# A hybrid RG-LRU and block-attention layer on one core: attention written out as a list of steps, with joined visits of TensorE

## The chip, the cores and the metric

The kernel runs on one NeuronCore of one Trainium2 chip. The metric is the device time of one execution in microseconds (us); the median of several runs is taken. Engines are named as in the profile: PE is TensorE, DVE is VectorE, ACT is ScalarE, POOL is GpSimd, SP is SyncE, which issues the DMAs.

## The reference, cut to what matters

One layer of a decoder for 512 tokens of width 1024, in float32:

```python
ada = silu(c) @ w_ada + b_ada;  shift, scale, gate = split(ada, 3)
h = rms_norm(x, norm_g) * (1 + scale) + shift
xl, gl, q, k, v, ga = split(h @ w_in, [512] * 6)
xl = causal_depthwise_conv(xl, conv_w, conv_b)
r = sigmoid(block_diag(xl, w_a) + b_a);  i = sigmoid(block_diag(xl, w_i) + b_i)
a = exp(-8 * r * softplus(-lam));  mult = sqrt(1 - a * a)       # mult[first token] = 1
h_t = a_t * h_(t-1) + mult_t * i_t * xl_t                        # the recurrence, a scan
y_lru = h_t * silu(gl)
q, k = rms_norm per head (8 heads of 64)
y_att = causal softmax attention(q, k, v) * silu(ga)
out = x + gate * (concat(y_lru, y_att) @ w_out)
```

The attention of the reference picks up to three past blocks of 256 keys for each query and its own block. With 512 tokens there are two blocks, so all past keys are always picked, and it is plain causal attention.

## The kernel before, in words

**Precision.** Each big product is made of three matmuls in the fast fp32 format: every operand is split into a high part (a copy, `split`, L272) and a low part (the difference), and high x high, high x low and low x high are summed in one PSUM bank.

**A planner sets the order.** The kernel doesn't issue instructions directly. Each step is an `op` (class `Plan`, L64) with a function that issues it, a cost in us for each engine that may run it, and the buffers that it reads and writes. `schedule` (L135) is a list scheduler: it repeatedly takes, among the steps whose inputs are done, the one that can start first; of those on the same engine that can start within `EPS_PICK` of it, the one with the smallest start plus `ALPHA` times due time. Due times come from the place of a TensorE step in the program text, and go backwards from each step to what it needs. A step that allocates a new SBUF slot may not start earlier than `window` (26 us) ahead of its due time; a step that writes into a slot which already exists has no such bound. Steps marked `bulk` (splits of weights) also leave ten of the 70 slots free. The planner keeps one more thing for TensorE: each step has a `mode` ("full" array, "row" for products on 64 rows, "col" for products on 64 columns, "col32"), and a step of another mode than the last is taken to start `SWITCH` later (L180). The order that comes out is the instruction order of every engine; semaphores do the rest at run time.

**PSUM.** There are eight banks. A step that opens a new use of a bank waits for every step of the bank's use before.

**Stages, in the order of TensorE.**
1. x is transposed and normed, ada is computed (TensorE for the first two k tiles, VectorE dot products for the six others, L443), h is made k tile by k tile from `gs` (L482 to L486) and split; xl and seven of eight tiles of the gates are accumulated over k (L515).
2. k, q and v for four token tiles (L617), with the RG-LRU gate products (L655) and the transposes of k and q (L724) in between. The RG-LRU chain behind the gate products (`gates`, L647 to L677): two tanh, an exp that gives a (L666), its square (L670), another tanh (L668), their product (L673); then `lru_sqrt` (L679), `lru_scan` (L685) and `lru_out` (L691).
3. Attention, for two pairs of query tiles a (a = 2 is the tiles 2 and 3, a = 0 the tiles 0 and 1) and four pairs of heads hp. `st_qk` (L748): S = q k^T for both heads of a pair at once, on the two row halves of the array, one step for each query tile, into banks 4 to 7. `softmax` (L773): mask and row maximum (L776, DVE), exp with row sum (L779, ACT), reciprocal (L782, DVE), scaling (L786 ACT, L788 POOL or DVE). `st_tr` (L792): transposes of P (L804) into banks 1 and 2 in turn, each copied out (pt). `st_pv` (L810): P v for both heads on the two column halves (L821), into bank 3; y = product with the attention gate (L824); after two head pairs y is split (ya).
4. In between as filler: five tiles of attention gates and the last RG-LRU gate (`g_tile`, L858), 24 matmuls each, in bank 0; the output gate's broadcast (`gate_bc`, L594), in bank 3.
5. The output product (`unit`, L830): for four token tiles and two halves of the columns, 24 matmuls each over y_lru (first 12) and y_att, then the multiplication by the gate, the residual and the store.

**The order of attention** before is a loop over six items (L917 to L940): the four head pairs of a = 2, then a = 0 in two items of two head pairs. Each turn puts S of the next item, one or two fills (a gate tile, and after the fourth item a unit), then the transposes and the pv of the item itself.

Of the kernel before, what the change touches and what calls it, by code (L numbers as in the profile page):

```python
# [29 lines left out]

NSLOT = 70
RESERVE = 10
SAME, SWITCH = 0.13, 0.1
EPS_PICK, ALPHA = 0.2, 0.1
NDV = 3
NPE = 2
# [27 lines left out]
class Plan:  # L64
# [70 lines left out]
    def schedule(self):  # L135
# [19 lines left out]
        while ready:  # L155
# [28 lines left out]
            if best is None:  # L184
# [1 line left out]
            s0, o0 = best  # L186
            e0 = o0.cand[0]
            o = min((r for r in ready if getattr(r, "cand", None) and r.cand[0] == e0 and r.cand[1] <= s0 + (EPS_PICK if s0 > T0 else EPS0)),
                    key=lambda r: r.cand[1] + (ALPHA if s0 > T0 else ALPHA0) * r.dl)
            for r in ready:  # L190
                if r is not o:
                    r.cand = None
# [46 lines left out]
def hybrid_layer_kernel(ctx: ExitStack, tc, x, small, call, bgate, wbd, wad, w1, wp, out):  # L239
# [23 lines left out]
        return op(fn, {"ACT": c_act(n, ap, psum), "DVE": c_dve(n, ap, psum, not psum)}, [src, *reads], [dst],  # L263
                  bulk=bulk, bias=bias)

    def tt(dst, d_ap, a, a_ap, b, b_ap, n, alu, psum=False, dve_only=False, rel=0.0):
        def fn(e):
            e.tensor_tensor(d_ap(), a_ap(), b_ap(), op=alu)  # L268
        costs = {"DVE": c_dve(n)} if psum or dve_only else c_tt(n)
        return op(fn, costs, [a, b], [dst], rel=rel)  # L270

    def split(src, s_ap, n, name, bulk=False, dve_only=False, rel=0.0):  # L272

# [157 lines left out]
    def load_ada(k):  # L431


        st = Buf(f"st{k}", "stage")
        for q in range(2):
            dma(lambda q=q: sp.dma_start(st.t[:, q * 1024:(q + 1) * 1024], wad[k, :, q * 1024:(q + 1) * 1024]), 0.5,
                [(st, q)], (DIP, 0.1, 0.1)[k] if k < 3 and q == 0 else 0.0)
        if k >= NPE:
            m = ada[k] = fixed(f"m{k}", [P, 2])
            for q in range(2):  # L440
                def dot(e, q=q):
                    v = st.t[:, q * 1024:(q + 1) * 1024]
                    dve.scalar_tensor_tensor(v, v, 1.0, cb.t, op0=MULT, op1=MULT, accum_out=m.t[:, q:q + 1])  # L443
                op(dot, {"DVE": c_dve(1024) + 0.15}, [cb], [(st, q), (m, q)])
            return
        acc = ada[k] = slot(f"ada{k}", n=256)
        part, p0 = (misc, 256) if k else (bank("adap0", 4), 0)

        def mm(q):
            for j in range(4):  # L450
                d = 4 * q + j
                pe.matmul(part.t[32 * j:32 * j + 32, p0:p0 + 256], csz.t[:, d, :], st.t[:, d * 256:(d + 1) * 256],
                          start=q == 0, stop=q == 1, tile_position=(0, 32 * j))
        key = (part, "sum")
# [16 lines left out]
    def gs_make(k):  # L471
        if k < NPE:
            acc = ada[k]

            def mm(e):
                for o in (0, 1):
                    pe.matmul(misc.t[:, 2 * k + o:2 * k + o + 1], acc.t[:, o * P:(o + 1) * P], ones.t[:, 0:1], start=True,
                              stop=True)
            op(mm, {"PE": 0.46}, [acc, ones], [(misc, k)], dl=T0 - 1.8 if k == 0 else T_[k] - 7.0)
        src = (misc, k) if k < NPE else ada[k]  # L480

        def mk(e):  # L482
# [164 lines left out]
    def gates(j, b_):  # L647
# [18 lines left out]
        op(lambda e: act.activation(aa_[j].t, tr.t, AF.Exp, bias=sn4.t[:, j:j + 1], scale=sn4.t[:, j:j + 1]),  # L666
           {"ACT": c_act(512, 2)}, [tr, sn4], [aa_[j]])
        op(lambda e: act.activation(t_.t, tr.t, AF.Tanh, bias=sp4.t[:, j:j + 1], scale=sp4.t[:, j:j + 1]),  # L668
           {"ACT": c_act(512, 2)}, [tr, sp4], [t_])
        tt(wv[j], lambda: wv[j].t, aa_[j], lambda: aa_[j].t, aa_[j], lambda: aa_[j].t, 512, MULT)  # L670

        def w_(e):
            dve.scalar_tensor_tensor(wv[j].t, wv[j].t, 1.0, t_.t, op0=ADD, op1=MULT)  # L673
            dve.memset(wv[j].t[:, 0:1], 1.0)
        op(w_, {"DVE": c_dve(512) + 0.07}, [t_], [wv[j]])
        op(lambda e: dve.scalar_tensor_tensor(ti[j].t, ti[j].t, 1.0, xc[j].t, op0=ADD, op1=MULT),
           {"DVE": c_dve(512)}, [xc[j]], [ti[j]])  # L677

    def lru_sqrt():  # L679
        def fn(e):  # L680
            for j in range(4):
                act.activation(wv[j].t, wv[j].t, AF.Sqrt, scale=1.0 / 16.0)
        op(fn, {"ACT": 4 * c_act(512) + 2.6}, [], [*wv])

    def lru_scan(j):  # L685
        w, c = wv[j], xc[j]
# [58 lines left out]
        ring.rotate(-1)  # L745
        return ring[-1]

    def st_qk(a, hps):  # L748

        for hp in hps:  # L750
            bb = {}
            for e_ in range(2):
# [1 line left out]
                    for t in (a + 1, a):  # L754
                        bb[t, e_] = (bank(f"S{t}{hp}{e_}", 4 + 2 * (t - a) + e_), 0)
                else:
                    b = bank(f"S{hp}{e_}", 4 + 2 * (hp - hps[0]) + e_)
                    bb[1, e_], bb[0, e_] = (b, 0), (b, 2 * P)
            for t in (a + 1, a):
                n = (t + 1) * P  # L760

                def fn(e, t=t, n=n, hp=hp, bb=bb):
                    for i, (x_, y_) in enumerate(((qTh, kTh), (qTh, kTl), (qTl, kTh))):
                        for e_ in range(2):
                            r, (b, c0) = slice(64 * e_, 64 * e_ + 64), bb[t, e_]
                            pe.matmul(b.t[:, c0:c0 + n], x_.t[r, hp, t * P:(t + 1) * P], y_.t[r, hp, 0:n],  # L766
                                      start=i == 0, stop=i == 2)
                op(fn, {"PE": c_mm(n, 3)}, [(qTh, t), (qTl, t)] + [(x_, i) for x_ in (kTh, kTl) for i in range(t + 1)],
                   [(bb[t, e_][0], t) for e_ in range(2)], mode="row")
                for e_ in range(2):  # L770
                    softmax(t, hp, e_, n, *bb[t, e_])

    def softmax(t, hp, e_, n, b, c0):  # L773
        st = fixed(f"st{t}{hp}{e_}", [P, 3])
        p_ = slot(f"P{t}{hp}{e_}")
        op(lambda e: dve.tensor_tensor_reduce(p_.t[:, :n], b.t[:, c0:c0 + n], maskf.t[:, 512 - n:], -1.0, -NEG,  # L776
                                              op0=ADD, op1=ALU.min, accum_out=st.t[:, 0:1]),
           {"DVE": c_dve(n) + 0.08}, [(b, t), maskf], [p_, (st, 0)])
        op(lambda e: act.activation(p_.t[:, :n], p_.t[:, :n], AF.Exp, bias=st.t[:, 0:1], scale=-1.0,  # L779
                                    accum_out=st.t[:, 1:2]),  # L780
           {"ACT": c_act(n, 2)}, [(st, 0)], [p_, (st, 1)])
# [28 lines left out]
    def st_pv(a, hp):  # L810
        if hp % 2 == 0:
            pv[a] = bank(f"pv{a}{hp}", 3)
            yy[a] = slot(f"y{a}{hp}")
        pt, b, y_, h0 = Tb.pop((a, hp)), pv[a], yy[a], 256 * (hp % 2)

        def fn(e):
            for kb in range(a + 2):
                n, o_ = (256, 0) if kb <= a else (128, 128)
                for e_ in range(2):
                    hd = 2 * hp + e_  # L820
                    pe.matmul(b.t[64 * e_:64 * e_ + 64, h0 + o_:h0 + o_ + n], vt[kb].t[:, hd * 64:(hd + 1) * 64],  # L821
                              pt[e_, kb // 2].t[:, 256 * (kb % 2):256 * (kb % 2) + n], start=kb == 0, stop=kb == a + 1)
        op(fn, {"PE": 0.26 + 0.435 * (a + 1)}, [*pt.values(), *vt[:a + 2]], [(b, hp)], mode="col")
        op(lambda e: dve.scalar_tensor_tensor(y_.t[:, h0:h0 + 256], b.t[:, h0:h0 + 256], 0.5,  # L824
                                              gga[hp].t[:, a * P:(a + 2) * P], op0=MULT, op1=MULT),
           {"DVE": c_dve(256)}, [(b, hp), gga[hp]], [(y_, hp)])
        if hp % 2 == 1:
            ya[a, hp // 2] = split(y_, lambda: y_.t, 512, f"ya{a}{hp}")
# [88 lines left out]
    items = [(2, (hp,)) for hp in range(4)] + [(0, (0, 1)), (0, (2, 3))]  # L917
    st_qk(*items[0])
    fill()
    for i in range(len(items)):  # L920
        if i + 1 < len(items):
            st_qk(*items[i + 1])
        fill()
        if i < 3:
            fill()
        if i == 2:
# [5 lines left out]
        a, hps = items[i]
        for hp in hps:
            st_tr(a, hp)
        for hp in hps:
            st_pv(a, hp)
        if i == 3:
# [87 lines left out]
```

## Time and profile before

| what | value |
|---|---|
| median of 3 runs | 237.19 us (237.05 to 237.79) |
| the profiled execution | 237.1 us |
| its span, first to last instruction | 235.3 us |
| granted clock of TensorE, mean | 0.998 |
| TensorE busy | 228.5 us, 97% of the span |
| VectorE busy | 173.0 us, 74% |
| ScalarE busy | 140.7 us, 60% |
| GpSimd busy | 55.4 us, 24% |
| HBM read, written | 35.43 MB, 2.10 MB |

How to read it: busy time is the time in which an instruction of the engine runs; a busy TensorE can still lose time between the starts of two matmuls, since matmuls are pipelined and their durations overlap. So its rate is read from the starts in the timeline. A group is a line of the kernel, an engine, an operation and its tiles, with the sum of its busy time and the mean of one. A wait is the idle time of an engine before an instruction, with what ended it. The stages lie at these times of the span: stage 1 until 56.5 us, k 56.5 to 81.9, q to 105.5, v to 129.9; attention with its fillers from 128.5 to 200.9; the rest of the output product until 232.1.

### The profile page before, as it was taken

How to read it: one execution, taken by the hardware profiler on the slowest of the kernel's cores; microseconds unless marked ns; L12 is line 12 of the kernel's file. 1: busy time of each engine (PE TensorE's matmuls, PEld its weight loads, DVE VectorE, ACT ScalarE, POOL GpSimd, SP SyncE). 2: the span in 40 equal slices, each digit the busy share in tenths (PEclk: the TensorE clock that was granted, in tenths of full speed). 3: DMA queues.
4: the chain of work that ended last, by engine and by line, in shares of the span. 5: the costliest groups of instructions: out<-in, count | busy, mean ns of one | idle time of the engine just before them, and what ended most of it. 6: DMA issues, size and time to landing. Idle time of an engine off the chain costs nothing.

```text
span 235.3 us, 3590 instructions
## 1 busy us (share of the span) xinstructions
PE 228.5 (97%) x1270; PEld 183.9 (78%) x1270; DVE 173.0 (74%) x399; ACT 140.7 (60%) x287; POOL 55.4 (24%) x56
## 2 busy tenths in 40 slices
PE   8799999999999999999999999999999999999994
PEld 8665888888878788888888778787777877788894
DVE  0778999979996767399745887597899894296221
ACT  5766555795487774342333399997998996140000
POOL 3300000000312844277020221447146320000001
PEclk9999999999999999999999999999999999999999
DMA  6999999958018005500654770001006031612411
GB/s 213 370 406 399 399 401 407 336 180 334 3 35 322 1 0 181 179 0 11 256 182 150 288 277 1 0 1 49 0 11 259 0 125 60 219 45 92 111 70 45
DMA packets 11879, 37.77 MB, mean 160 GB/s; under 512 B 1362, under 2 KB 3922, under 8 KB 9812
## 3 DMA queue, kind: packets, MB, share of 16 engines
q1 hardware_dynamic: 11860, 37.53, 44.2%
q8 instruction: 10, 0.16, 0.3%
q14 instruction: 9, 0.07, 0.1%
HBM read 35.43 MB, written 2.10 MB: 159 GB/s over the span
## 4 chain that ended last, share of the span: by engine, by line
PE 83%; DMA 9%; DVE 3%; ACT 2%; SPq 1%; issue 0%; DVEq 0%
PE u L843 19%; PE k L617 9%; PE g L867 9%; PE q L617 9%; PE xl L515 9%; PE gl L515 7%; PE v L617 6%; PE PT L804 4%; PE pv L821 4%; DMA st<-in_wad_dram 4%; DMA c<-in_call_dram 3%; PE S L766 3%; DVE ga L591 2%; DMA wg<-in_wp_dram 2%; PE pr L655 1%; ACT P L779 1%
## 5 line engine op out<-in xcount | busy, mean ns | idle before, releaser
L779 ACT ACTIVATE P<-P,st 128x512 f32<-128x512 f32 (+3 forms) x32 | 17.6, 556 | 3.5 <-DVE st L776 3.5
L268 DVE TENSOR_TENSOR o<-u,gbc 128x512 f32<-128x512 f32 (+1 forms) x8 | 5.3, 658 | 14.5 <-PE u L843 14.5
L788 POOL TENSOR_SCALAR P<-P,st 128x384 f32<-128x384 f32 (+3 forms) x13 | 9.0, 699 | 25.6 <-DVE st L782 25.6
L776 DVE CUSTOM_DVE_ANT_0 P<-S,maskf 128x512 f32<-128x512 f32 (+3 forms) x32 | 14.3, 481 | 0.9 <-PE g L867 0.9
L591 DVE SCALAR_TENSOR_TENSOR ga<-wg,cs,ga 128x512 f32<-128x512 f32 x16 | 12.8, 837 | 2.0 <-DMA wg<-in_wp_dram 2.0
L443 DVE SCALAR_TENSOR_TENSOR st<-st,cb 128x1024 f32<-128x1024 f32 x12 | 14.3, 1219 | 0.0
L268 POOL TENSOR_TENSOR xcs0l<-xc,xcs0h 128x512 fp32r<-128x512 f32 x1 | 1.3, 1294 | 50.6 <-ACT xcs0h L258 50.6
L258 ACT ACTIVATE pt<-PT 128x384 f32<-128x384 f32 (+1 forms) x23 | 11.1, 525 | 3.4 <-PE PT L804 3.2
L804 PE MATMUL PT<-ident,P 128*128 128x128 f32 x80 | 11.4, 277 | 0.3 <-ACT P L786 0.3
L804 PEld LDWEIGHTS PT<-ident,P 128*128 128x128 f32 x80 | 9.0, 141 | 3.1 <-issue 1.1
L821 PE MATMUL pv<-pt,vt 128*64 128x256 f32 (+1 forms) x96 | 10.0, 351 | 0.0
L786 ACT ACTIVATE P<-P,st 128x128 f32<-128x128 f32 (+3 forms) x19 | 9.5, 544 | 0.0
L496 ACT ACTIVATE hf<-xs,gs 128x512 f32<-128x512 f32 x8 | 6.5, 809 | 5.0 <-DVE gs L485 5.0
L712 POOL TENSOR_TENSOR msk<-msk,nhalf 128x8 f32<-128x8 f32 x4 | 6.6, 1647 | 12.3 <-DVE po L361 9.5
L821 PEld LDWEIGHTS pv<-pt,vt 128*64 128x64 f32 x96 | 6.4, 137 | 4.0 <-issue 1.2
L268 POOL TENSOR_TENSOR w_1l<-wp,w_1h 128x512 fp32r<-128x512 f32 x3 | 4.6, 1537 | 20.5 <-ACT w_1h L258 13.8
L268 DVE TENSOR_TENSOR w_0l<-wp,w_0h 128x512 fp32r<-128x512 f32 x11 | 8.1, 737 | 1.5 <-ACT w_0h L258 1.5
L258 ACT ACTIVATE qTh<-Tq 128x512 fp32r<-128x512 f32 x4 | 2.4, 598 | 11.3 <-PE Tq L724 11.3
L712 POOL TENSOR_TENSOR msq<-msq,nhalf 128x8 f32<-128x8 f32 x4 | 7.8, 1951 | 5.5 <-DVE msq L710 5.3
L268 POOL TENSOR_TENSOR o<-xr,o 128x256 f32<-128x256 f32 x1 | 0.7, 737 | 34.6 <-DVE o L268 34.6
L636 DVE SCALAR_TENSOR_TENSOR xc<-xl,sm,xc 128x511 f32<-128x511 f32 (+2 forms) x12 | 8.1, 740 | 0.3 <-ACT xc L633 0.3
L423 PE MATMUL warm<-warm 128*128 128x128 bf16 x72 | 6.6, 272 | 1.0 <-DVE warm L305 1.0
(719 smaller groups left out, 776.9 us busy)
## 6 DMA issues: line engine op xcount, KB each, us to landing
wp<-in_wp_dram SPq DMA_DIRECT2D x12, 1024.0 KB, 4.8
st<-in_wad_dram SPq DMA_DIRECT2D x16, 512.0 KB, 7.5
wg<-in_wp_dram SPq DMA_DIRECT2D x4, 1024.0 KB, 4.8
x<-in_x_dram SPq DMA_DIRECT2D x4, 512.0 KB, 6.0
wa<-in_w_dram SPq DMA_DIRECT2D x8, 256.0 KB, 7.7
xr<-in_x_dram SPq DMA_DIRECT2D x7, 256.0 KB, 2.9
out_dram<-o SPq DMA_DIRECT2D x7, 256.0 KB, 2.0
wb<-in_w_dram SPq DMA_DIRECT2D x8, 192.0 KB, 7.5
```

Of the source, the lines that this page charges most:

```text
L268: e.tensor_tensor(d_ap(), a_ap(), b_ap(), op=alu)
L443: dve.scalar_tensor_tensor(v, v, 1.0, cb.t, op0=MULT, op1=MULT, accum_out=m.t[:, q:q + 1])
L515: pe.matmul(acc.t, a.t[:, c0:c0 + P], b.t, start=k == 0 and i == 0, stop=k == KT - 1 and i == 2)
L591: dve.scalar_tensor_tensor(gacc[hf].t, w, cs.t[:, d:d + 1], gacc[hf].t, op0=MULT, op1=ADD)
L617: pe.matmul(acc.t, hx[kt].t[:, a * P:(a + 1) * P], wx.t, start=s0, stop=s1)
L712: op(lambda e: pool.tensor_tensor(m.t, m.t, nhalf.t, op=ALU.pow), {"POOL": 1.65}, [nhalf], [m])
L776: op(lambda e: dve.tensor_tensor_reduce(p_.t[:, :n], b.t[:, c0:c0 + n], maskf.t[:, 512 - n:], -1.0, -NEG, op0=ADD, op1=ALU.min, accum_out= ...
L779: op(lambda e: act.activation(p_.t[:, :n], p_.t[:, :n], AF.Exp, bias=st.t[:, 0:1], scale=-1.0, accum_out=st.t[:, 1:2]), {"ACT": c_act(n, 2 ...
L804: pe.transpose(b.t[:, o_:o_ + P], p_.t[:, kb * P:(kb + 1) * P], ident.t)
L821: pe.matmul(b.t[64 * e_:64 * e_ + 64, h0 + o_:h0 + o_ + n], vt[kb].t[:, hd * 64:(hd + 1) * 64], pt[e_, kb // 2].t[:, 256 * (kb % 2):256 * ...
L843: pe.matmul(b.t[:, :cn], y_.t[:, c0:c0 + P], w.t[:, cw:cw + cn], start=kt == 0 and i == 0, stop=kt == KT - 1 and i == 2)
L867: pe.matmul(b.t, wx.t[:, c0:c0 + P], hx[kt].t, start=kt == 0 and p == 0, stop=kt == KT - 1 and p == 2)
```

## The change

Four things, all in the kernel's text.

- **Attention as a list of steps.** The loop is replaced by a string `ORDER`. `S20` is a visit of S for a = 2 and head pair 0, `T20` the transposes of it, `P20` a pv visit, `P02+P03` two visits joined in one step. `F` is a fill in bank 0, `F3` a fill in bank 3. `G` is the broadcast of the output gate, `W` the end of the RG-LRU group and the loads of the output weights, `U` puts four units on the list of fillers. Fills that find nothing to do do nothing. The list was found off line by replaying plans.
- **Joined visits.** `st_qk` and `st_pv` become `qk_part` and `pv_part`, and `visit` makes one TensorE step of all their matmuls. S of both query tiles of a head pair is now one step (two before), and S of a = 0 is a visit of its own for each head pair, in banks 4 and 5 for even and 6 and 7 for odd pairs.
- **The RG-LRU chain opened ahead.** The exp and the square have a window of 200 us in place of 26; the second tanh overwrites `tr` in place of a new slot.
- **Costs of the planner.** `SWITCH` is 0.2 in place of 0.1. `TURN` adds 0.3 to the key of a TensorE step of another mode. The costs of the dots, the gate tanh, the square roots and the mask pass are set to traced durations. `gs` for k from 2 on runs on ScalarE (two one-column activations) in place of VectorE.

The diff, cut to its core:

```diff
+ORDER = ("S20 F3 S22 F F3 F3 S21 T20 T21 F3 P20 F S23 F W S00 T22 T23 P21 S01 G T01 P22 T00 F3 S03 F S02 P23 "
+         "P00 T03 F P01 U T02 P02+P03")
+TURN = 0.3
+AHEAD = 200.0
-SAME, SWITCH = 0.13, 0.1
+SAME, SWITCH = 0.13, 0.2
...
-                    key=lambda r: r.cand[1] + (ALPHA if s0 > T0 else ALPHA0) * r.dl)
+                    key=lambda r: r.cand[1] + (ALPHA if s0 > T0 else ALPHA0) * r.dl
+                    + (TURN if e0 == "PE" and r.mode != mode else 0.0))
...
-                op(dot, {"DVE": c_dve(1024) + 0.15}, [cb], [(st, q), (m, q)])
+                op(dot, {"DVE": c_dve(1024) + 0.09}, [cb], [(st, q), (m, q)])
...
+            if e is act:
+                for o in range(2):
+                    act.activation(g[:, o:o + 1], m[:, o:o + 1], AF.Identity, bias=ga_.t[:, k, o:o + 1],
+                                   scale=gm.t[:, k, o:o + 1])
+                return
...
-        op(mk, {"DVE": 0.3}, [src, gm, ga_], [(gs, k)], sbuf=False)
+        op(mk, {"DVE": 0.27} if k < NPE else {"ACT": 0.45}, [src, gm, ga_], [(gs, k)], sbuf=False)
...
-           {"ACT": c_act(512, 2)}, [tr, sn4], [aa_[j]])
-        op(lambda e: act.activation(t_.t, tr.t, AF.Tanh, bias=sp4.t[:, j:j + 1], scale=sp4.t[:, j:j + 1]),
-           {"ACT": c_act(512, 2)}, [tr, sp4], [t_])
-        tt(wv[j], lambda: wv[j].t, aa_[j], lambda: aa_[j].t, aa_[j], lambda: aa_[j].t, 512, MULT)
+           {"ACT": c_act(512, 2)}, [tr, sn4], [aa_[j]], window=AHEAD)
+        op(lambda e: act.activation(tr.t, tr.t, AF.Tanh, bias=sp4.t[:, j:j + 1], scale=sp4.t[:, j:j + 1]),
+           {"ACT": c_act(512, 2)}, [sp4], [tr])
+        tt(wv[j], lambda: wv[j].t, aa_[j], lambda: aa_[j].t, aa_[j], lambda: aa_[j].t, 512, MULT, window=AHEAD)
...
-           {"DVE": c_dve(n) + 0.08}, [(b, t), maskf], [p_, (st, 0)])
+           {"DVE": c_dve(n) + 0.005}, [(b, t), maskf], [p_, (st, 0)])
...
+    def visit(*todo):
+        parts = [(mode, (qk_part if mode == "row" else pv_part)(a, hps)) for mode, a, hps in todo]
+        fns, reads, writes, after = ([x for _, p_ in parts for x in p_[i]] for i in (0, 2, 3, 4))
+        turns = sum(u[0] != v[0] for u, v in zip(parts, parts[1:]))
+        op(lambda e: [fn(e) for fn in fns], {"PE": sum(p_[1] for _, p_ in parts) + SWITCH * turns}, reads, writes,
+           mode=parts[0][0])
+        for fn in after:
+            fn()
...
-    def fill():
+    def fill(bank_=0):
+        u_ring[0] = bank_
         if not filler and groups:
             groups.pop(0)()
         if filler:
             filler.popleft()()
...
+    for step in ORDER.split():
+        if step[0] == "F":
+            fill(int(step[1:] or 0))
+        elif step == "G":
             gate_bc((3, 3))
+        elif step == "W":
             for j in range(4):
                 lru_out(j)
             for dh in range(2):
                 wo.append(w_piece(13 + 2 * dh) + w_piece(14 + 2 * dh))
+        elif step == "U":
             filler += [lambda t=t, dh=dh: unit(t, dh) for t in (3, 2) for dh in (0, 1)]
+        elif step[0] == "T":
+            for hp in step[2:]:
+                st_tr(int(step[1]), int(hp))
+        else:
+            visit(*[("row" if v[0] == "S" else "col", int(v[1]), tuple(int(c) for c in v[2:])) for v in step.split("+")])
```

More of the change, by code (lines that the diff above doesn't have):

```diff
@@ L264, in copy, with tt @@
                   bulk=bulk, bias=bias)
-    def tt(dst, d_ap, a, a_ap, b, b_ap, n, alu, psum=False, dve_only=False, rel=0.0):
+    def tt(dst, d_ap, a, a_ap, b, b_ap, n, alu, psum=False, dve_only=False, rel=0.0, window=None):
         def fn(e):
@@ L269, in tt @@
         costs = {"DVE": c_dve(n)} if psum or dve_only else c_tt(n)
-        return op(fn, costs, [a, b], [dst], rel=rel)
+        return op(fn, costs, [a, b], [dst], rel=rel, window=window)
     def split(src, s_ap, n, name, bulk=False, dve_only=False, rel=0.0):
@@ L656, in gates @@
         op(mm, {"PE": c_mm(512, 3)}, [wbh, wbl, xs_h, xs_l], pb, mode="row")
-        tr, t_ = slot(f"tr{j}"), slot(f"t_{j}")
+        tr = slot(f"tr{j}")
         ti[j], aa_[j], wv[j] = slot(f"ti{j}"), slot(f"aa{j}"), slot(f"wv{j}")
@@ L664, in th @@
                                    bias=hb.t[r, 2 * j + q:2 * j + q + 1], scale=0.5)
-                op(th, {"ACT": c_act(512, 1, True)}, [(pb[q], i), hb], [(dst, q)])
+                op(th, {"ACT": 0.69}, [(pb[q], i), hb], [(dst, q)])
         op(lambda e: act.activation(aa_[j].t, tr.t, AF.Exp, bias=sn4.t[:, j:j + 1], scale=sn4.t[:, j:j + 1]),
-           {"ACT": c_act(512, 2)}, [tr, sn4], [aa_[j]])
-        op(lambda e: act.activation(t_.t, tr.t, AF.Tanh, bias=sp4.t[:, j:j + 1], scale=sp4.t[:, j:j + 1]),
-           {"ACT": c_act(512, 2)}, [tr, sp4], [t_])
-        tt(wv[j], lambda: wv[j].t, aa_[j], lambda: aa_[j].t, aa_[j], lambda: aa_[j].t, 512, MULT)
+           {"ACT": c_act(512, 2)}, [tr, sn4], [aa_[j]], window=AHEAD)
+        op(lambda e: act.activation(tr.t, tr.t, AF.Tanh, bias=sp4.t[:, j:j + 1], scale=sp4.t[:, j:j + 1]),
+           {"ACT": c_act(512, 2)}, [sp4], [tr])
+        tt(wv[j], lambda: wv[j].t, aa_[j], lambda: aa_[j].t, aa_[j], lambda: aa_[j].t, 512, MULT, window=AHEAD)
         def w_(e):
-            dve.scalar_tensor_tensor(wv[j].t, wv[j].t, 1.0, t_.t, op0=ADD, op1=MULT)
+            dve.scalar_tensor_tensor(wv[j].t, wv[j].t, 1.0, tr.t, op0=ADD, op1=MULT)
             dve.memset(wv[j].t[:, 0:1], 1.0)
-        op(w_, {"DVE": c_dve(512) + 0.07}, [t_], [wv[j]])
+        op(w_, {"DVE": c_dve(512) + 0.07}, [tr], [wv[j]])
         op(lambda e: dve.scalar_tensor_tensor(ti[j].t, ti[j].t, 1.0, xc[j].t, op0=ADD, op1=MULT),
@@ L682, in fn @@
                 act.activation(wv[j].t, wv[j].t, AF.Sqrt, scale=1.0 / 16.0)
-        op(fn, {"ACT": 4 * c_act(512) + 2.6}, [], [*wv])
+        op(fn, {"ACT": 3.5}, [], [*wv])
     def lru_scan(j):
@@ L746, in take, with qk_part @@
         return ring[-1]
-    def st_qk(a, hps):
+    def qk_part(a, hps):
+        fns, cost, reads, writes, after = [], 0.0, [], [], []
         for hp in hps:
@@ L756, in st_qk @@
                 else:
-                    b = bank(f"S{hp}{e_}", 4 + 2 * (hp - hps[0]) + e_)
+                    b = bank(f"S{hp}{e_}", 4 + 2 * (hp % 2) + e_)
                     bb[1, e_], bb[0, e_] = (b, 0), (b, 2 * P)
@@ L767, in fn @@
                                       start=i == 0, stop=i == 2)
[L768 to L771, printed above, removed]
+                fns.append(fn)
+                cost += c_mm(n, 3)
+                reads += [(qTh, t), (qTl, t)] + [(x_, i) for x_ in (kTh, kTl) for i in range(t + 1)]
+                writes += [(bb[t, e_][0], t) for e_ in range(2)]
+                after += [lambda t=t, hp=hp, e_=e_, n=n, bb=bb: softmax(t, hp, e_, n, *bb[t, e_]) for e_ in range(2)]
+        return fns, cost, reads, writes, after
     def softmax(t, hp, e_, n, b, c0):
@@ L808, in st_tr, with pv_part, fn, y_make @@
                 Tb.setdefault((a, hp), {})[e_, c] = pt
[L810 to L828, printed above, removed]
+    def pv_part(a, hps):
+        fns, cost, reads, writes, after = [], 0.0, [], [], []
+        for hp in hps:
+            if hp % 2 == 0:
+                pv[a] = bank(f"pv{a}{hp}", 3)
+                yy[a] = slot(f"y{a}{hp}")
+            pt, b, y_, h0 = Tb.pop((a, hp)), pv[a], yy[a], 256 * (hp % 2)
+            def fn(e, hp=hp, pt=pt, b=b, h0=h0):
+                for kb in range(a + 2):
+                    n, o_ = (256, 0) if kb <= a else (128, 128)
+                    for e_ in range(2):
+                        hd = 2 * hp + e_
+                        pe.matmul(b.t[64 * e_:64 * e_ + 64, h0 + o_:h0 + o_ + n], vt[kb].t[:, hd * 64:(hd + 1) * 64],
+                                  pt[e_, kb // 2].t[:, 256 * (kb % 2):256 * (kb % 2) + n], start=kb == 0,
+                                  stop=kb == a + 1)
+            def y_make(hp=hp, b=b, y_=y_, h0=h0):
+                op(lambda e: dve.scalar_tensor_tensor(y_.t[:, h0:h0 + 256], b.t[:, h0:h0 + 256], 0.5,
+                                                      gga[hp].t[:, a * P:(a + 2) * P], op0=MULT, op1=MULT),
+                   {"DVE": c_dve(256)}, [(b, hp), gga[hp]], [(y_, hp)])
+                if hp % 2 == 1:
+                    ya[a, hp // 2] = split(y_, lambda: y_.t, 512, f"ya{a}{hp}")
+            fns.append(fn)
+            cost += 0.26 + 0.435 * (a + 1)
+            reads += [*pt.values(), *vt[:a + 2]]
+            writes.append((b, hp))
+            after.append(y_make)
+        return fns, cost, reads, writes, after
@@ L915, in fill @@
             filler.popleft()()
[L917 to L926, printed above, removed]
+    for step in ORDER.split():
+        if step[0] == "F":
+            fill(int(step[1:] or 0))
+        elif step == "G":
             gate_bc((3, 3))
+        elif step == "W":
             for j in range(4):
@@ L931, in hybrid_layer_kernel @@
                 wo.append(w_piece(13 + 2 * dh) + w_piece(14 + 2 * dh))
[L932 to L937, printed above, removed]
-            filler += [lambda t=t, dh=dh: unit(t, dh) for t in (3, 2) for dh in (0, 1)]
+        elif step == "U":
+            filler += [lambda t=t, dh=dh: unit(t, dh) for t in (3, 2) for dh in (0, 1)]
+        elif step[0] == "T":
[3 more added lines that the diff above has]
+            visit(*[("row" if v[0] == "S" else "col", int(v[1]), tuple(int(c) for c in v[2:])) for v in step.split("+")])
     while filler:
```

## The prediction

> **What bounds the kernel now.** I read the page first (busy times, slices), then the waits of TensorE, then the busy times by stretch, and last the timeline of TensorE instruction by instruction. The profiled execution took 237.1 us, of which 235.3 are the span; 1.8 us lie around it. The median of the three runs is 237.19, so a sum made against the profiled execution stands for the median within 0.1.
>
> ```profile
> PE 228.5 (97%) x1270; PEld 183.9 (78%) x1270; DVE 173.0 (74%) x399; ACT 140.7 (60%) x287; POOL 55.4 (24%) x56
> PEclk9999999999999999999999999999999999999999
> ```
> ```profile
> 20.00:56.00 36.00, 35.69 (x158) 29.21 (x158) 34.23 (x71) 22.70 (x40) 0.00 (x0) 1.00 0.93 348
> 82.00:105.00 23.00, 23.00 (x111) 19.05 (x110) 15.54 (x26) 11.55 (x20) 10.47 (x8) 1.00 0.27 92
> 105.00:131.00 26.00, 26.00 (x124) 21.54 (x123) 16.85 (x27) 8.84 (x16) 6.97 (x5) 1.00 0.45 162
> 126.00:201.00 75.00, 74.69 (x469) 57.87 (x468) 59.01 (x165) 62.73 (x149) 24.35 (x24) 1.00 0.28 98
> ```
> ```profile
> PE PT L804 <- ACT P L786: 0.3, 1, 0.3
> ```
> The columns of the stretches are stretch and its length, then busy time of PE, PEld, DVE, ACT, POOL. TensorE works without a break: in the attention stretch, 126 to 201 us, it is busy 74.69 of 75.00 us, and the missing 0.31 is the single wait of a transpose for a scaled P. A change of order cannot win by removing waits there. It can only win what TensorE loses while it counts as busy. That is seen in the starts of its instructions (start, duration, line, operation):
>
> ```profile
> 131.45 0.39 PE L867 MATMUL g<-h3l,w_0h 128*128 128x512 f32 x1
> 131.68 0.39 PE L867 MATMUL g<-h3h,w_0l 128*128 128x512 f32 x1
> 132.00 0.50 PE L766 MATMUL S<-kTh,qTh 64*128 64x512 f32 x2
> 132.33 0.40 PE L766 MATMUL S<-kTl,qTh 64*128 64x512 f32 x2
> 133.16 0.34 PE L766 MATMUL S<-kTh,qTl 64*128 64x384 f32 x2
> 133.43 0.50 PE L867 MATMUL g<-h4h,w_1h 128*128 128x512 f32 x1
> 133.76 0.39 PE L867 MATMUL g<-h4l,w_1h 128*128 128x512 f32 x1
> ```
> ```profile
> 138.59 0.47 PE L867 MATMUL g<-h0h,w_2h 128*128 128x512 f32 x1
> 138.91 0.39 PE L867 MATMUL g<-h0l,w_2h 128*128 128x512 f32 x1
> 139.13 0.39 PE L867 MATMUL g<-h0h,w_2l 128*128 128x512 f32 x1
> ```
> A 512-column matmul follows another after 0.23 us (131.45 to 131.68). Where the full array turns to the two row halves of the S products, the gap is 0.32 (131.68 to 132.00), and the first S pair takes 0.33 (132.00 to 132.33): 0.09 plus 0.10 lost. On the way back the first g takes 0.33 as well (133.43 to 133.76). So a turn between array modes costs **0.19 us**. Smaller, 0.09 to 0.10, is what the first matmul behind a group of transposes loses (138.59 to 138.91 is 0.32, the next gap 0.22).
>
> **Counting the turns.** Between the S visit at 132.00 and the last pv at 199.45 the timeline has nine stretches of row mode (S) and six of column mode (pv); pieces of the chain of waits show how they lie:
>
> ```profile
> 160.95 0.89 PE S L766 x3
> 161.84 0.48 PE PT L804 x3
> 162.32 0.72 PE S L766 x6
> ...
> 174.04 0.55 PE S L766 x6
> 174.59 1.66 PE pv L821 x16
> 176.25 1.17 PE S L766 x18
> 177.42 0.91 PE PT L804 x7
> 178.34 0.84 PE S L766 x9
> 179.17 0.90 PE u L843 x3
> 180.07 1.66 PE pv L821 x16
> 181.73 0.84 PE S L766 x12
> ...
> 199.45 1.45 PE pv L821 x16
> ```
> Fifteen stretches have thirty ends, less three where a row and a column stretch touch (twice around 174.59, once at 181.73): **27 turns**, 27 x 0.19 = 5.1 us. Two more things are seen: the S of one head pair was torn in two by transposes (160.95 and 162.32), and three unit matmuls at 179.17 stood alone between S and pv.
>
> **The change, part by part.**
>
> *Joined visits and the written order.* S of both query tiles of a head pair becomes one TensorE step, so it can no longer be torn: 2 turns less. The list, read with its empty fills left out (five gate tiles exist, so from the sixth F to U a fill does nothing), gives S20, S22, S21 alone; P20 S23 S00 together; P21 S01 together; P22 alone; S03 S02 P23 P00 together; P01; P02+P03. That is six row and six column stretches, 24 ends less three contacts: 21 turns. I don't believe all of it. S00 writes banks 4 and 5, which S23 has just filled and which come free only when the mask passes have read them, so something else will go between them (2 turns back); P00 allocates bank 3 anew behind P23, so it waits for the product of y, and may be split off as well (another 2). So 21 to 25 turns; I take 23, since the first of these two waits is the longer one. Saved: 4 x 0.19 = **0.76 us** (ends 0.38 and 1.14).
>
> The Trainium skill, "TensorEngine Tiling (Array Packing)", Key Properties, says that a change of tiling mode drains the array, and "TensorE: Matmul & The Clock Gate", Part 2, puts the drain at about 128 cycles. An estimate from these two pages is 0.05 us for a turn, by which four turns would be worth 0.2 and the sum below would be 236.9; the rows show 0.19, and they decide.
>
> *Durations and TURN in the planner.* They issue nothing. They change which ready step is taken first; their effect is the order above and the one wait of 0.31, which goes: **0.31 us**. What is late next is set by the softmax (below).
>
> *RG-LRU chain opened ahead.* With AHEAD, and with the second tanh written over tr (so no new buffer and no window), exp, square, tanh, product, square root and scan run as soon as their inputs are there, some 60 us earlier.
>
> ```profile
> L666 ACT ACTIVATE aa<-tr,sn 128x512 f32<-128x512 f32 x4 | 3.2, 811 | 0.0
> L668 ACT ACTIVATE t<-tr,sp 128x512 f32<-128x512 f32 x4 | 3.2, 808 | 0.1
> L682 ACT ACTIVATE wv<-wv 128x512 f32<-128x512 f32 x4 | 2.2, 623 | 0.0
> L682 ACT ACT_TABLE_LOAD x1 | 1.3, 1283 | 0.0
> L673 DVE SCALAR_TENSOR_TENSOR wv<-wv,t 128x512 f32<-128x512 f32 x4 | 2.7, 682 | 0.0
> L688 DVE TENSOR_TENSOR_SCAN xc<-aa,wv 128x512 f32<-128x512 f32 x4 | 5.7, 1450 | 0.0
> ```
> These rows are of 131 to 201 us. ScalarE loses 3.2 + 3.2 + 2.2 + 1.3 = 9.9 us of its 62.73 there, VectorE 2.7 + 5.7 = 8.4 of 59.01. TensorE didn't wait for either, so this alone is worth 0; it is room for a denser order. The work lands between 82 and 131 us, where ScalarE is idle 11.45 + 17.16 = 28.6 us and VectorE 7.46 + 9.15 = 16.6. It fits. It is queued ahead of the evictions of q and k and of the splits of v's weights; if one of those came behind a scan, TensorE would wait at most for one scan, 1.45 us. I take 0.
>
> *gs on ScalarE for k of 2 and more.* Two one-column activations replace two one-column VectorE operations.
>
> ```profile
> L398 ACT ACTIVATE r<-ss,eps 128x1 f32<-128x1 f32 x4 | 1.2, 295 | 0.1
> ```
> At 0.30 each that is 0.6 us per k on an engine that is busy 22.70 of 36.00 us in that stretch, and it relieves VectorE, busy 34.23. TensorE idles 0.31 in the stretch, so the bounds are -0.3 and +0.6 (one pair in the way of the first h); I take 0, as gs is made two k ahead. The dot's duration in the planner issues nothing.
>
> *Gate tiles in bank 3.* Two in a row on one bank wait for its tanh and product. S21 and T20 stand in the list beside them. Without that cover it is about one copy and one mask pass, 0.53 + 0.48 = 1.0 us, from the rows below. I charge **0.3** for all such bank and softmax waits, by the size of the one wait that the trace shows.
>
> Sum: 237.1 - 0.76 - 0.31 + 0.3 = **236.3 us**. With the ends of each (turns 0.38 to 1.14, bank waits 0 to 1.0, gs -0.3 to +0.6) the case reaches from 235.4 to 237.2.
>
> **The rivals.**
>
> *The softmax behind S23 starves TensorE (slower).* All five gate tiles are spent before P20. From S23 until P23 the list has no filler: units need P23, and only the RG-LRU part of the first, 12 matmuls or 12 x 0.23 = 2.8 us, can run ahead.
>
> ```profile
> L776 DVE CUSTOM_DVE_ANT_0 P<-S,maskf 128x512 f32<-128x512 f32 (+3 forms) x32 | 14.3, 481 | 0.9 <-PE g L867 0.9
> L779 ACT ACTIVATE P<-P,st 128x512 f32<-128x512 f32 (+3 forms) x32 | 17.6, 556 | 3.5 <-DVE st L776 3.5
> L786 ACT ACTIVATE P<-P,st 128x128 f32<-128x128 f32 (+3 forms) x19 | 9.5, 544 | 0.0
> L258 ACT ACTIVATE pt<-PT 128x384 f32<-128x384 f32 (+1 forms) x23 | 11.1, 525 | 3.4 <-PE PT L804 3.2
> ```
> From S23's end to P23's inputs: four mask passes 1.92, the last exp 0.56, its scaling 0.54, two copies 1.05: 4.1 us at least, and twice that, 8.2, if each step queues behind another. The cover is T22 at 2 x 0.91, P21 and P22 at 1.66 each, S00 and S01 at 0.84 each: 6.8 us, 9.6 with the unit's part. It decides from the point where the chain is longer than 6.8 and the unit's part isn't ready: 1.4 us, and again at the last head pairs, 2.8. That gives 237.7 to 239.1, say 238.4. For it: ScalarE is 84% busy there. Against it: the 9.9 us taken off ScalarE.
>
> *The turns come back (no change).* A list scheduler takes what is ready; if S and pv are ready at different times, the contacts of the list don't happen, 25 to 27 turns stay, and only the 0.31 goes, against some 0.3 of new waits: 236.7 to 237.4, say 237.0. For it: bank 3 and banks 4 and 5, as above.
>
> *All of it (faster by more).* 21 turns, 1.14 us, the 0.31, and the transposes laid together so that eight losses of 0.10 behind them go too: 237.1 - 2.25 = 234.9.
>
> *The clock drops.* A stretch of transposes alone, T22 with T23, is 4 x 0.91 = 3.6 us; if the clock fell to half in it, the pv and the unit part behind it would take twice their time, 1.66 + 2.8 = 4.5 us more: 240.8. The trace grants the full clock in all forty slices, the stretches of transposes included. The Trainium skill, "TensorE: Matmul & The Clock Gate", Part 4, says that transposes don't count as activity for the clock gate; no run here shows a stretch long enough to test it.
>
> **How the numbers follow.** A measurement of this kernel tells 0.3%, 0.7 us, from no change, so faster means below 236.48. Forecast 50% (three quarters of its reach lie below 236.48, the rest within), turns come back 24%, starved 15%, all of it 8%, clock 3%. Faster: 0.5 x 0.75 + 0.08 and a little of the second = 0.48. Slower: 0.15 + 0.03 and a little of the second = 0.21. Same: 0.31. The range takes in the forecast, the turns that come back, nearly all of the larger gain and the lower half of the starved case: 235.0 to 238.4. The forecast's own range is 235.4 to 237.2.
>
> **What would show it.** Right: 21 to 25 turns, S always in whole visits, TensorE idle under 0.5 us between 126 and 201, exp, root and scan before 131, and the end of the last pv earlier by about 0.8. Wrong: TensorE waiting for a scaled P, a copied PT or bank 3 between S23 and P23 by a microsecond or more; a gap before 126 in front of Tq or v; or as many turns as before. If the time falls by more than 2 us, something ahead of 126 has moved, which I have costed at nothing.

## The result, and the profile after

The changed kernel takes **235.67 us** (median of 4 runs, 235.62 to 235.73), the kernel before 237.19: a ratio of 0.9931, 95% interval 0.991 to 0.9951, or 1.5 us less. The forecast was 236.3. The profiled execution of the changed kernel took 235.73 us, its span is 233.9.

Where the time came from is seen by laying the two timelines side by side. The first matmul of v starts at 105.54 us in both. The last matmul of all starts at 231.80 before and at 230.42 after:

```profile
231.80 0.28 PE L843 MATMUL u<-wl7l,ya03h 128*128 128x256 f32 x1
```
```profile
230.42 0.28 PE L878 MATMUL u<-wl7l,ya03h 128*128 128x256 f32 x1
```
That is 1.38 us less, all of it behind 105.5. Next the busy times by stretch of the changed kernel (stretch and length, then PE, PEld, DVE, ACT, POOL), and its waits of TensorE in attention:

```profile
82.00:105.00 23.00, 23.00 (x116) 18.75 (x113) 19.03 (x35) 19.64 (x31) 8.83 (x8) 1.00 0.28 92
105.00:131.00 26.00, 26.00 (x124) 21.54 (x123) 23.87 (x31) 10.42 (x19) 12.03 (x8) 1.00 0.36 127
126.00:201.00 75.00, 74.55 (x475) 59.07 (x474) 54.02 (x158) 50.82 (x130) 25.27 (x27) 1.00 0.31 107
```
```profile
PE gb L610 <- DVE y L843: 0.5, 1, 0.5
```
TensorE waits a little more than before: 0.5 us in one place (the output gate's broadcast, for y) in place of 0.3. ScalarE is busy 50.82 us of the 75 in place of 62.73: the RG-LRU chain has gone ahead, to 82 to 131 us, where ScalarE was 20.4 us busy and is now 30.1. The gain isn't in waits. It is in the order of TensorE; pieces of the chain of waits of the changed kernel:

```profile
133.44 1.43 PE S L778 x12
...
141.21 1.43 PE S L778 x11
...
149.75 1.42 PE S L778 x10
...
157.61 1.43 PE S L778 x11
...
167.00 1.53 PE S L778 x24
168.53 3.23 PE pv L838 x32
...
177.29 3.18 PE pv L838 x32
...
182.62 1.53 PE S L778 x24
184.15 1.45 PE pv L838 x16
...
191.96 1.45 PE pv L838 x16
193.41 37.31 PE u L878 x186
```
Between the first S and the last pv the timeline has six stretches of row mode where there were nine, and four of column mode where there were six. Two pv visits stand together at 168.53 and again at 177.29 (32 matmuls where there were 16), two S visits at 167.00 and at 182.62. With two contacts of a row and a column stretch that is 20 - 2 = **18 turns in place of 27**. No S is torn (a visit of 12 matmuls shows as 10 or 11 where the trace lacks records).

### The profile page after: what moved, and what is told of

Same layout as the page of the kernel before. It is cut to its first block, busy times and chain, and to the rows that moved or that the text cites. A ratio compares the mean times of both kernels' runs of the same rounds, so it can differ in the third digit from the quotient of the medians.

```text
span 233.9 us, 3618 instructions
## 1 busy us (share of the span) xinstructions
PE 227.0 (97%) x1270; PEld 184.1 (79%) x1270; DVE 173.7 (74%) x393; ACT 139.1 (59%) x289; POOL 56.8 (24%) x60
## 4 chain that ended last, share of the span: by engine, by line
PE 89%; DMA 7%; SPq 1%; DVE 1%; ACT 0%; issue 0%
PE u L878 19%; PE g L902 12%; PE q L627 9%; PE k L627 9%; PE v L627 9%; PE xl L525 9%; PE gl L525 7%; PE pv L838 4%; DMA st<-in_wad_dram 4%; PE S L778 4%; PE PT L818 4%; DMA c<-in_call_dram 3%; PE pr L665 1%; PE Tk L734 1%; PE Tq L734 1%; SPq L296 1%
## 5 line engine op out<-in xcount | busy, mean ns | idle before, releaser
L802 POOL TENSOR_SCALAR P<-P,st 128x128 f32<-128x128 f32 (+3 forms) x18 | 12.4, 696 | 24.3 <-DVE st L796 11.8
L263 ACT ACTIVATE pt<-PT 128x384 f32<-128x384 f32 (+1 forms) x24 | 11.6, 532 | 2.2 <-PE PT L818 2.2
L273 DVE TENSOR_TENSOR w_1l<-wp,w_1h 128x512 fp32r<-128x512 f32 x12 | 8.9, 743 | 0.9 <-ACT w_1h L263 0.7
L838 PE MATMUL pv<-pt,vt 128*64 128x256 f32 (+1 forms) x96 | 9.5, 348 | 0.0
L273 DVE TENSOR_TENSOR w_0l<-wp,w_0h 128x512 fp32r<-128x512 f32 x12 | 9.1, 754 | 0.5 <-ACT w_0h L263 0.3
L800 ACT ACTIVATE P<-P,st 128x384 f32<-128x384 f32 (+3 forms) x14 | 7.9, 590 | 1.0 <-DVE st L796 1.0
L722 POOL TENSOR_TENSOR msq<-msq,nhalf 128x8 f32<-128x8 f32 x4 | 6.9, 1730 | 6.1 <-DVE msq L720 6.1
L273 POOL TENSOR_TENSOR w_2l<-wp,w_2h 128x512 fp32r<-128x512 f32 x4 | 5.5, 1387 | 10.5 <-ACT w_2h L263 5.9
```

What stands on the lines that cost most here:

```text
L722: op(lambda e: pool.tensor_tensor(m.t, m.t, nhalf.t, op=ALU.pow), {"POOL": 1.65}, [nhalf], [m])
```

## The experiments

**What a turn costs.** Four kernels put the same small matmul 24 times into the tail of the changed kernel, behind every third matmul of three units, where TensorE never waits. They differ in the form of that matmul alone; each kernel has one of these four lines:

```diff
+                if dm is not None:
+                    pe.matmul(dm.t[:, :256], qTh.t[0:64, 0, 0:P], kTh.t[0:64, 0, 0:256], start=True, stop=True)   # e1: 64 rows
+                    pe.matmul(dm.t[:, :256], qTh.t[:, 0, 0:P], kTh.t[:, 0, 0:256], start=True, stop=True)         # e2: full array
+                    pe.matmul(dm.t[0:64, :256], qTh.t[:, 0, 0:64], kTh.t[:, 0, 0:256], start=True, stop=True)     # e3: 64 columns
+                    pe.transpose(dm.t[:, :P], maskf.t[:, 0:P], ident.t)                                           # e4: transpose
```


> The changed kernel with 24 more matmuls of 256 columns on 64 rows, one behind every three matmuls of three units in the tail, where TensorE never waits. Each makes two turns, 48 in all. Theory (a turn costs 0.19 us): against the same matmuls on the full array (the next run) 48 x 0.19 = 9.1 us more. Rival (a turn is nearly free, about 0.05 us, and the gain came from elsewhere): 2.4 us more. The added result is not used.

> The control of the run before: the same 24 matmuls on the full array, no turn. Both theories: 24 x 0.12 = 2.9 us over the changed kernel, 238.6.

> The same 24 matmuls into 64 columns. Theory: a turn to column mode costs what one to row mode costs, so 9.1 us over the control. Rival: column mode is cheaper, since the pv visits in the trace show only 0.05 lost in their first matmul and not 0.10: (0.09 + 0.05) x 24 + 0.19 x 24 = 7.9 us.

> 24 transposes of 128x128 in the same places, full array. Theory: each costs its 0.11 and 0.10 in the matmul behind it: 24 x 0.21 = 5.0 us over the changed kernel, 240.7. Rival (a transpose costs no more than it takes): 2.6, 238.3.

Measured, in one run each: 249.54, 239.00, 239.12 and 238.75 us. One place of each, from the timelines (start, duration), in the order 64 rows, full array, 64 columns, transpose:

```profile
221.04 0.39 PE L878 MATMUL u<-w_1l,yl1h 128*128 128x512 f32 x1
221.36 0.38 PE L881 MATMUL dm<-kTh,qTh 64*128 64x256 f32 x1
221.67 0.50 PE L878 MATMUL u<-w_2h,yl2h 128*128 128x512 f32 x1
222.01 0.39 PE L878 MATMUL u<-w_2h,yl2l 128*128 128x512 f32 x1
```
```profile
213.09 0.39 PE L878 MATMUL u<-w_1l,ya01h 128*128 128x512 f32 x1
213.32 0.28 PE L881 MATMUL dm<-kTh,qTh 128*128 128x256 f32 x1
213.44 0.40 PE L878 MATMUL u<-w_2h,ya03h 128*128 128x512 f32 x1
213.67 0.40 PE L878 MATMUL u<-w_2h,ya03l 128*128 128x512 f32 x1
```
```profile
213.12 0.39 PE L878 MATMUL u<-w_1l,ya01h 128*128 128x512 f32 x1
213.34 0.28 PE L881 MATMUL dm<-kTh,qTh 128*64 128x256 f32 x1
213.46 0.40 PE L878 MATMUL u<-w_2h,ya03h 128*128 128x512 f32 x1
213.70 0.40 PE L878 MATMUL u<-w_2h,ya03l 128*128 128x512 f32 x1
```
```profile
212.87 0.39 PE L878 MATMUL u<-w_1l,ya01h 128*128 128x512 f32 x1
213.10 0.27 PE L881 MATMUL dm<-ident,maskf 128*128 128x128 f32 x1
213.13 0.48 PE L878 MATMUL u<-w_2h,ya03h 128*128 128x512 f32 x1
213.45 0.40 PE L878 MATMUL u<-w_2h,ya03l 128*128 128x512 f32 x1
```
Read the differences of the starts. On the full array the three gaps are 0.23, 0.12, 0.23. On 64 rows they are 0.32, 0.31, 0.34: 0.09, 0.19 and 0.11 more, 0.39 for two turns. **A row turn costs 0.20 us**, here where nothing else happens; the rival of 0.05 falls. (The 10.5 us between the two times are more than 24 x 0.39 = 9.4. The rest lies ahead of the added matmuls: the first matmul of v starts at 106.85 in the run on 64 rows and at 105.60 in the control. The granted clock between 6 and 18 us was 0.85 to 0.87 in the one and 1.00 in the other.)

The other two were surprises. The matmul into 64 columns loses nothing: both the theory (9.1 us) and its rival (7.9) fall, the difference was 0.1. And the transpose shows 0.23, 0.03, 0.32: the last two make 0.35, a matmul's 0.23 and the transpose's own 0.12. The 0.32 behind transposes is not lost; the transpose's time is only seen one gap later. So the theory (240.7) falls, and the rival (238.3) is the nearer one with 238.75 measured.

**Why a pv visit costs a turn and that matmul doesn't.** In the trace of before the first pv gap is 0.09 late as well, and pv differs from the added matmul in two ways: plain fp32 operands, and both column halves. One kernel with one kind in each of four units:

```diff
+    unit(1, 0, dm=("pair", dmb))       # plain fp32, both column halves
+    unit(1, 1, dm=("high", dmb))       # plain fp32, upper half
+    unit(0, 0, dm=("low32", dmb))      # plain fp32, lower half
+    unit(0, 1, 0, 256, dm=("full32", dmb))   # plain fp32, full array
```


> Why the single matmuls into 64 columns cost no turn in an earlier run while a pv visit does. In the tail of the changed kernel, one kind in each of four units, eight times each, all in plain fp32 as pv is: (1) a pair into both column halves, (2) one into the lower half, (3) one on the full array, (4) one into the upper half (behind 256-column matmuls). Theory A (the second column half makes the turn): 1 and 4 lose about 0.3 us for each place beside the matmul's own time, 2 and 3 nothing. Theory B (the change between the fast fp32 format and plain fp32 makes it): all four lose. Theory C (only a matmul of part of the columns in plain fp32): 1, 2 and 4 lose, 3 does not. The added results are not used.

(In the kernel the kinds stand in the order of the diff: upper half second, full array last.) The upper half, then the full array behind 256-column matmuls, where a gap without a turn is 0.12:

```profile
223.46 0.40 PE L878 MATMUL u<-w_2l,yl2h 128*128 128x512 f32 x1
223.79 0.65 PE L887 MATMUL dm<-maskf,ident 128*64 128x256 f32 x2
224.36 0.50 PE L878 MATMUL u<-w_3h,yl3h 128*128 128x512 f32 x1
224.70 0.39 PE L878 MATMUL u<-w_3h,yl3l 128*128 128x512 f32 x1
```
```profile
245.34 0.28 PE L878 MATMUL u<-w_2l,yl2h 128*128 128x256 f32 x1
245.46 0.59 PE L891 MATMUL dm<-maskf,ident 128*128 128x256 f32 x2
245.70 0.47 PE L878 MATMUL u<-w_3h,yl3h 128*128 128x256 f32 x1
246.01 0.28 PE L878 MATMUL u<-w_3h,yl3l 128*128 128x256 f32 x1
```
On the full array the fp32 matmul enters without delay (0.12) and takes 0.24 + 0.31 - 0.12 = 0.43 us, for its two passes (x2 in the row). Into the upper half it enters 0.10 late (0.33), takes 0.57, and the next gap is 0.34: 0.10 + 0.14 + 0.11 = 0.35 us lost. The lower half and the pair show the same gaps. So theory C holds: it is neither the second half nor the number format alone, but a matmul of part of the columns in plain fp32, **0.17 us a turn**. Why the fast format escapes isn't settled.

**Each part alone.** The planner's price on turns alone, in the kernel before:

```diff
-SAME, SWITCH = 0.13, 0.1
+SAME, SWITCH = 0.13, 0.2
+TURN = 0.3        # and its term in the key of schedule; nothing else
```


> The kernel before with only SWITCH 0.2 and TURN 0.3: no list of steps, no joined visits, the RG-LRU chain as it was. TensorE's program has 21 turns from the first S on, in place of 27. Theory (the gain is the turns, 0.19 us each): 237.2 - 6 x 0.19 = 236.05, plus whatever new wait TensorE meets. Rival (the gain is the room that the RG-LRU chain leaves on ScalarE): no change, 237.2.

Measured 236.32 us, ratio 0.9949 (0.9926 to 0.9972). With no list, no joined visits and no moved chain it brings 0.9 us of the 1.5; the rival falls. The sum behind the theory doesn't close, though. In the trace the 0.3 us wait of the kernel before is gone and no new one in attention is shown, so six turns and that wait should give 1.45 us behind the start of v; TensorE is only 0.75 faster there. Two groups of seven transposes, at 149.45 with S behind it and at 172.18 with the gate's broadcast behind it, take 0.99 and 0.98 us; in the kernel before, such groups take 0.85 and 0.78. That is 0.34 of the missing 0.7. The rest is not placed.

The list and the joined visits, with the planner's old price:

```diff
-SAME, SWITCH = 0.13, 0.2
+SAME, SWITCH = 0.13, 0.1
-TURN = 0.3
+TURN = 0.0
```


> The changed kernel with SWITCH back at 0.1 and TURN at 0: the list and the joined visits, planned without a price on turns. 23 turns in place of 18. Theory: 235.67 + 5 x 0.19 = 236.6. Rival (the list itself is the gain, whatever the planner makes of it): 235.7.

Measured 236.72 us, ratio 0.9973 (0.9955 to 0.9991), near the 236.6 of the theory. The same list gives 23 turns without the price and 18 with it, so the list is only half of the order. That the number fits is in part luck: this kernel also waits 1.1 us in attention, 0.6 more than the changed kernel, which the theory didn't count and which would make 237.2.

```profile
PE PT L818 <- POOL P L802: 0.8, 1, 0.8
PE pv L838 <- DVE g L653: 0.3, 1, 0.3
```

The RG-LRU chain: alone in the kernel before, and taken out of the changed kernel.

```diff
-           {"ACT": c_act(512, 2)}, [tr, sn4], [aa_[j]])
+           {"ACT": c_act(512, 2)}, [tr, sn4], [aa_[j]], window=200.0)     # e6; e7 is the reverse
...
-        op(lambda e: act.activation(t_.t, tr.t, AF.Tanh, bias=sp4.t[:, j:j + 1], scale=sp4.t[:, j:j + 1]),
+        op(lambda e: act.activation(tr.t, tr.t, AF.Tanh, bias=sp4.t[:, j:j + 1], scale=sp4.t[:, j:j + 1]),
```


> The kernel before with only the RG-LRU chain opened ahead. TensorE's program has 29 turns in place of 27 and 6 in place of 8 returns from transposes to the full array. Theory: 237.2 + 2 x 0.19 - 2 x 0.1 = 237.4, no gain. Rival (room on ScalarE): the 0.31 us wait goes and more, 236.5.

> The changed kernel with the RG-LRU chain as it was before (window 26, own slot for the second tanh). 20 turns in place of 18, 7 returns from transposes in place of 9. Theory: 235.67 + 2 x 0.19 - 2 x 0.1 = 235.85, plus waits if the denser order needs the room on ScalarE; I expect such waits, 0.5 us or more. Rival (room is not needed): 235.85 and no new wait of TensorE.

Measured: alone 238.94 us, ratio 1.0079 (1.0052 to 1.0107), slower; taken out 240.01, ratio 1.0127 (1.0076 to 1.0177), slower as well. For the second the theory named the cause and missed the size: 4 us where 0.5 or more was expected. ScalarE's timeline of that kernel shows it, and then two waits of TensorE:

```profile
164.35 0.72 ACT L800 ACTIVATE P<-P,st 128x512 f32<-128x512 f32 x1
165.08 1.28 ACT L692 ACT_TABLE_LOAD   x1
166.37 2.19 ACT L692 ACTIVATE wv<-wv 128x512 f32<-128x512 f32 x4
168.59 1.28 ACT L652 ACT_TABLE_LOAD   x1
169.88 0.60 ACT L652 ACTIVATE g<-g 128x512 f32<-128x512 f32 x1
170.37 0.97 ACT L263 ACTIVATE pt<-PT 128x512 f32<-128x512 f32 x2
```
```profile
PE PT L818 <- ACT pt L263: 1.8, 1, 1.8
PE pv L838 <- DVE st L796: 1.4, 1, 1.4
```
The square roots with their two table loads hold ScalarE for 4.8 us, from 165.08 to 169.88; the copies of the transposed P stand behind them, and the transposes behind the copies; that is the first wait, which ends at 171.02. The second ends at 186.16, at the last head pairs, and hangs on the softmax there. The denser list has no gate tile left behind 165.6 us to fill the time. In the changed kernel the roots run at 98 us and cost nothing.

For the chain alone no theory fitted: 237.4 or 236.5 was expected. Once more, for its trace:

> The kernel before with only the RG-LRU chain opened ahead, once more for its trace: it took 238.9 where 237.4 was expected from 29 turns. Theory (new waits of TensorE, 1.5 us in all, because the loop's order brings S and P closer together when ScalarE is free): waits of PT or pv of over 1 us in the attention stretch and none before 126 us. Rival (the chain collides with the evictions of q and v): the waits lie between 82 and 131 us.

```profile
PE PT L804 <- ACT P L786: 1.4, 1, 1.4
```
```profile
131.50 3.93 DVE L591 SCALAR_TENSOR_TENSOR ga<-wg,cs,ga 128x512 f32<-128x512 f32 x3
135.35 0.68 DVE L776 CUSTOM_DVE_ANT_0 P<-S,maskf 128x512 f32<-128x512 f32 x1
```
It took 239.38. The first transposes wait 1.4 us, as in the trace of the first of these two runs, and none of the new waits lies between 82 and 131 us. VectorE shows why: S is done at 133.9, but the first mask pass starts at 135.35, behind three steps of the output gate's sum. In the kernel before, the same three steps stand there too:

```profile
130.60 3.15 DVE L591 SCALAR_TENSOR_TENSOR ga<-wg,cs,ga 128x512 f32<-128x512 f32 x3 [2.05 <-DMA wg<-in_wp_dram]
133.68 0.68 DVE L776 CUSTOM_DVE_ANT_0 P<-S,maskf 128x512 f32<-128x512 f32 x1
```
So the moved chain didn't put them there. It made them start 0.9 us later (0.5 later against the first S), at the end of a row of scans and products, and they took 0.8 us longer. To test that this delay is the wait, the last eight steps of the sum were planned later:

```diff
-                    op(stt, {"DVE": c_dve(512, 1)}, [st, cs], [gacc[hf]])
+                    op(stt, {"DVE": c_dve(512, 1)}, [st, cs], [gacc[hf]], rel=134.5 if i >= 2 else 0.0)
```


> The kernel before with the RG-LRU chain ahead, and the last eight steps of the output gate's sum planned not before 134.5 us, so that on VectorE they stand behind the first mask passes. 29 turns as in the run without it. Theory (the lone chain loses because the scans moved the gate's sum in front of the first mask pass, and the first transposes wait 1.4 us for it): that wait goes, 237.4 to 238.0. Rival (any order of the loop waits somewhere when the chain is ahead): the wait comes back at another place and it stays at 238.9 or more.

```profile
PE PT L804 <- ACT P L786: 0.3, 1, 0.3
PE gb L600 <- DVE y L824: 0.2, 1, 0.2
```
The wait falls from 1.4 to 0.3, as the theory had it, and the profiled execution took 237.79. But the median is 238.30 (237.70 to 240.34), ratio 1.0059 (1.0022 to 1.0096), between theory and rival, and the interval overlaps that of the chain alone. The later steps also changed the order of S and pv from 145 us on: the third S, whole in the chain alone, is torn here. So the queue behind the gate's sum is shown as the cause of that wait; that it is the whole loss of the chain alone is not. By the count, the two turns more that both kernels have (29) would be a second part, 0.38 us at 0.19 each.

**Fewer turns still.** Another list, and TURN 0.45:

```diff
-TURN = 0.3
+TURN = 0.45
+ORDER = ("S20 F3 F3 S21 F T20 F3 F3 T21 P20 F S22 P21 S23 S00 W T23 F F T22 S01 "
+         "G P22 F3 P23 S03 T00 T01 P00 S02 F3 U P01 T02 P02 T03 P03")
```


> The changed kernel with another list and TURN 0.45: 17 turns in place of 18, row stretches 6 and column stretches 4 as before the edit, one contact more. Theory: 235.67 - 0.19 = 235.5, less the 0.49 wait of the gate broadcast if it is covered. Rival (the turns that are left are cheap contacts): 235.7.

Measured 235.74 us, ratio 0.9939 (0.9923 to 0.9956): the same as the changed kernel. So the rival stands as far as the runs can tell: one contact more is worth at most the 0.2 us that they don't resolve. The wait of the gate broadcast did go, but a wait of 0.5 us for a copied P came in its place. No version beat the changed kernel.

## Why the prediction was right, and where it was off

The direction, the mechanism and the range (235.0 to 238.4) held, and so did the forecast's own range (235.4 to 237.2), near its lower end. The saving was 1.5 us where 0.8 was forecast. Two figures behind the ranges and chances were wrong: the upper ends add up to 237.1 - 0.38 - 0.31 + 1.0 + 0.6 = 238.0, not 237.2, and of 235.4 to 237.2 six tenths, not three quarters, lie below 236.48, so that "faster" should have had about 0.4. Point by point:

- *A turn costs 0.19 us.* Shown, and now by itself: 0.20 to and from row mode, 0.17 to and from column mode in plain fp32. The row decided rightly against the 0.05 drawn from the Trainium skill ("TensorEngine Tiling (Array Packing)", Key Properties, with "TensorE: Matmul & The Clock Gate", Part 2). That a change of mode costs, as the first of these pages of the Trainium skill says, agrees with the 64-row runs; the fast-format matmul into 64 columns, which lost nothing, doesn't show it. As a sum, 0.19 for each turn and the waits shown, it misses TensorE's time behind the start of v by 0.1 to 0.5 us in the changed kernel and the five other orders whose traces are here, and by 0.7 in the planner's price alone.
- *23 turns.* This is the term that was mis-sized: 18 were made. I counted which contacts of the list would break (S23 with S00, P23 with P00), and both did. I didn't count what the planner's TURN would join that the list keeps apart: P20 with P21, P22 with P23, P00 with P01, S00 with S01. I had written that the durations and TURN have an effect only through the list's order and one wait; SWITCH and TURN alone save six turns and 0.9 us. Nine turns at 0.19 are 1.7 us where I put 0.76.
- *Waits.* -0.31 and +0.3 in the sum; -0.31 and +0.46 in the trace, at bank 3's gate broadcast. 237.1 - 1.71 + 0.15 gives 235.5 against the 235.73 of the profiled execution. TensorE idled 0.45 us between 126 and 201, under the 0.5 that I had named. The other sign, the last pv ending about 0.8 earlier, was no measure: it ends at 193.3 in place of 200.8, as the order of pv and units has changed.
- *The RG-LRU chain is worth 0 by itself, and is room.* Half right. It is room, and the list needs it: without it 4.3 us are lost. But moved alone it isn't 0; it costs 1.7. The cover that I named (VectorE's 16.6 idle microseconds up to 131 us) did hold until 131, but not for all of the chain: the last scan of the changed kernel starts at 139.9, not before 131. That the changed kernel escapes because its first transposes come 15 us after the first S, where the old loop has them 6 us after, fits the traces; no run tests it alone.
- *gs on ScalarE, the dots, bank 3 for gate tiles.* Nothing of them shows in the time: the first matmul of k starts at 56.49 before and 56.50 after, that of v at 105.54 in both. Between these two the order has changed (q starts 1.8 us earlier, the RG-LRU gate products 4 us later), at no gain or loss. No gate tile waits for bank 3; the gate broadcast does, above.
- *The larger gain* counted 0.10 behind each group of transposes as a loss. That was misread; the runs with transposes show that it is their own time.
- *Starvation behind S23* didn't happen, but the run without the chain is just that case: its waits of 1.8 us between S23 and P23 and of 1.4 at the last head pairs lie where the rival put them. It needed ScalarE blocked for 4.8 us.
- *The clock* stayed at full speed. The long stretch of transposes didn't arise, as T22 and T23 were broken up, so the Trainium skill's rule on transposes remains untested here.

## What to carry to other kernels

When an engine is busy all the time, look at the starts of its instructions and not at its busy share: the loss sits in gaps of a tenth of a microsecond at each change of mode, and counting the changes and the waits gave the gain here to a few tenths of a microsecond. A price in the scheduler can do more than a list written by hand: alone they gave 0.9 and 0.5 us, together 1.5. A move off the critical path is only free if you follow its last instruction, on every queue, to where it comes out, and it may be worthless alone and necessary together with a denser order.

## What the runs showed of the hardware that was not expected

A matmul into 64 of 128 columns in the fast fp32 format costs no turn (gaps 0.22, 0.12, 0.24); in plain fp32 it loses 0.35 us in and out. A transpose's own time shows up in the gap behind the next start (0.03, then 0.32).

Steps of the output gate's sum, 0.74 us each as a rule, took up to 1.78 where GpSimd ran beside them:

```profile
L591 DVE SCALAR_TENSOR_TENSOR ga<-wg,cs,ga x16: 732/742/1784, 107.0 to 145.1; 128x512 f32<-128x512 f32 x16
```
This row is from the chain alone (shortest, median and longest in ns). The Trainium skill, "SBUF — State Buffer", section "SBUF: two separate sides", says that VectorE operations with two SBUF inputs and GpSimd operations that read SBUF lock each other out of a shared port for a whole instruction. The trace agrees with that: GpSimd's own product beside them took 2.26 us in that run, against 1.28 for the same form elsewhere. No run here takes GpSimd's work away, so this cause isn't shown by itself.
